# Feed-forward products summed in PSUM: one bank for p1, p6, p7, p4, another for p5, p3

## The chip, the cores and the metric

The kernel runs on one core of one Trainium2 chip. The metric is the device time of one execution in microseconds (us); lower is better. The engines are TensorE (PE in the profile; PEld is its loading of weights), VectorE (DVE), ScalarE (ACT), GpSimd (POOL) and SyncE (SP), which here only issues DMAs. Each engine and each queue works in order.

## The reference

One step of a one-layer encoder in float32: a combined input projection, two groups of attention heads, an output projection, and then a feed-forward block, for 512 prompt tokens and 8 x 16 sample tokens, 640 in all. The change touches only the feed-forward block:

```python
def merge_and_ffn(x, oa, ob, norm_grp_a, norm_grp_b, w_out, norm_ffn, w_gate, w_up, w_down):
    o = jnp.concatenate([rmsnorm(oa, norm_grp_a), rmsnorm(ob, norm_grp_b)], axis=-1)
    x = x + o @ w_out
    h = rmsnorm(x, norm_ffn)
    return x + (jax.nn.silu(h @ w_gate) * (h @ w_up)) @ w_down
```

The model width is 2048 and the inner width of the block is 5632. A final rmsnorm follows.

## The kernel before

**Precision.** Every operand is split into a high and a low part of a short float type (`split`, lines 137 to 139: ScalarE makes the high part on line 138, VectorE the low part on line 139), and a product is three matmuls (`mm3`, lines 145 to 149): high x high, high x low, low x high. One matmul has 128 x 128 weights and 320 columns, half of the 640 tokens.

**A quartet.** The three matrix products of the block use a scheme of the Strassen-Winograd kind. Two blocks of output rows by two halves of the tokens make four results c11, c21, c12, c22 of 128 x 320; seven products p1 to p7 take the place of eight. `quartet` (line 815) makes them. It loads four blocks of weights b11, b12, b21, b22 (each up to 8 x 128 columns; `get`, line 833, with the load on line 835), forms differences of them (VectorE on lines 848 and 850, GpSimd on 852 and 859) and yields one finished product after another. Each `product` (line 820) splits its weights into a pair of tiles from the list H and runs 3 x k matmuls into one PSUM bank, where k is 8 in gate and up and 5 or 6 in down. The right operands are seven sums of activations, prepared beforehand.

The results, with P for a product:

- c11 = P1 + P2
- c12 = (P1 + P6) + P5 + P3
- c22 = (P1 + P6 + P7) + P5
- c21 = (P1 + P6 + P7) + P4

Before, each product is a PSUM sum of its own: p1 and p5 lie in the two banks of one tile x, p6 and p3 in the two banks of a tile y (pool `dn`, two tiles of two banks, line 134), p7, p2 and p4 in single banks (pool `at`, four tiles of one bank, line 131). The order is p1, p6, p7, p2, p5, p4, p3. All the sums above are made by VectorE, by the helper `add` (line 869), from a bank and a tile in SBUF.

**Gate and up.** For each of 22 pairs of row blocks (line 899) there is one quartet on w_gate and one on w_up, 44 in all. ScalarE copies p1 out of PSUM (line 908), and seven adds follow (lines 910 to 921). c11 and c21 are the halves of tile y[0], c12 and c22 of y[1]. Then a gate pair is scaled and goes through SiLU (lines 931 to 933), and an up pair is multiplied by it (line 937), summed up for the down products (lines 941 to 944) and stored to `act_d` in memory (lines 945 to 947). In the first quartet (`start`) the last of the activation sums are prepared in between (`prep`); in the last (`end`) `free` gives back tiles as the products finish and fetches the first activations.

**Down.** 32 steps (`step`, line 959), each a quartet over 5 or 6 pairs; each of eight output pairs q is met four times, at t = q, q + 8, q + 16, q + 24. The results are kept in SBUF in two tiles per q, loaded with the residual. Besides, a sum u of P1 + P6 over the four visits is kept in a further tile per two q; in the last visit (`last`) it is added to c21, c22 and c12 (lines 988 to 990). That makes ten VectorE adds in a step, one less in the first eight steps, where ScalarE copies P1 to u (line 982), and three more in the last eight. Between steps the activations of a pair that comes into use are fetched and split (`fetch`, line 873: ScalarE on 881, VectorE or GpSimd on 882). Steps 30 and 31 are run in two parts: "early" (p1, p6, p7, p5, p4), in which c21 and c22 become final, then "late" (p2, p3). Between and behind them the final norm is computed (`squares`, line 1020; `rstd_steps`, line 183) and the output scaled and stored (`finish`, line 1031, with lines 1037 to 1041).

**Order.** The program is written as if each step were done in turn; a scheduler then orders each engine's queue by priority in program order and by when it expects operands to be there. So splits run one or two products ahead of the matmuls. Tiles in SBUF come from lists (S of 128 x 640, W of 128 x 1024, H taken out of W) and are handed on in the order in which they come free.

## Time and profile before

| what | value |
| --- | --- |
| median of three runs | 2685.09 us (2684.39 to 2686.73) |
| the profiled execution | 2686.44 us, of which its span 2684.7 us |
| mean granted clock of TensorE in it | 0.986 |
| VectorE adds of line 869 from a `dn` bank | 358, 163.9 us busy |
| VectorE adds of line 869 from an `at` bank | 262, 123.1 us busy |
| gate and up | from about 985 to 2085 us of the span |
| down | from about 2085 us to the end |

In a row of busy times by stretch, the first two numbers are the stretch and its length, then each engine's busy time with the count of its instructions in brackets (PE, PEld, DVE, ACT, POOL), then the granted clock of TensorE, the busy share of the DMA engines and GB/s. In a row of waits, the waiting engine with the tile and line of its instruction stands first, then what released it, then the total in us, the number of waits and the longest one. In a row of groups, the line, engine and operation, the tiles (written <- read, `dn` and `at` being PSUM), the shape and the count stand ahead of the bar, then the busy time in us and the mean in ns, then the idle time before them with its releasers. In a row of the timeline, the start and the duration in us come first.

### The profile page before, as it was taken

What the parts mean: (1) busy time and instruction counts of PE and PEld (TensorE: products, weight loads), DVE (VectorE), ACT (ScalarE), POOL (GpSimd) and SP (SyncE); (2) the same over time, 40 slices, a digit from 0 to 9 for tenths busy, and PEclk for the clock granted to TensorE, in tenths of its full rate; (3) what the DMA queues carried; (4) which work ended last, traced back from release to release, by engine and by line L of the source; (5) the groups of instructions that cost most, each with busy time, mean ns of one, the idle gap of its engine ahead of it and who ended that gap; (6) DMA issues with size and microseconds to landing.
All of it is one profiled execution on the core that took longest, in us unless ns stands there. A gap on an engine that the chain in (4) does not pass through costs nothing.

```text
span 2684.7 us, 44841 instructions
## 1 busy us (share of the span) xinstructions
PE 2602.1 (97%) x17565; PEld 2545.6 (95%) x17565; DVE 1930.3 (72%) x2956; ACT 1081.6 (40%) x1759; POOL 785.4 (29%) x564
## 2 busy tenths in 40 slices
PE   7999999999999999999999999999999999999986
PEld 7999999899899999999999999999999899999986
DVE  7565565766775787766667676667678888888897
ACT  4343343444543543333333333333334444444443
POOL 3000000001211223333333433433335534344354
PEclk8999999999999999999999999999999999999998
DMA  5222222344566433333333333333335644444344
GB/s 162 91 74 85 86 81 86 121 127 129 191 195 206 141 130 101 106 121 102 108 117 98 122 107 112 113 104 107 117 105 169 217 136 125 132 135 130 108 114 139
DMA packets 154147, 332.23 MB, mean 124 GB/s; under 512 B 18064, under 2 KB 69264, under 8 KB 153936
## 3 DMA queue, kind: packets, MB, share of 16 engines
q1 hardware_dynamic: 153936, 329.38, 38.8%
q8 instruction: 138, 2.26, 0.4%
q14 instruction: 73, 0.60, 0.1%
HBM read 274.38 MB, written 54.20 MB: 122 GB/s over the span
## 4 chain that ended last, share of the span: by engine, by line
PE 64%; DVE 5%; DMA 2%; issue 2%; ACT 1%; POOL 0%; SPq 0%; DVEq 0%; POOLq 0%; ACTq 0%
PE dn L149 13%; PE dn L147 13%; PE dn L148 13%; PE at L149 8%; PE at L148 8%; PE at L147 8%; DVE W L139 2%; DVE S L869 1%; DMA S<-act_d 1%; DMA W<-w_down 1%; DVE S L1040 1%; PE at L259 0%; DVE S L882 0%; DVE W L850 0%; ACT W L138 0%
## 5 line engine op out<-in xcount | busy, mean ns | idle before, releaser
L147 PE MATMUL dn<-S,W 128*128 128x320 f32 x3694 | 1163.5, 315 | 14.6 <-DVE S L869 5.6
L149 PE MATMUL dn<-S,W 128*128 128x320 f32 x3694 | 1154.4, 313 | 15.1 <-DVE W L139 14.9
L148 PE MATMUL dn<-S,W 128*128 128x320 f32 x3694 | 1152.7, 312 | 1.1 <-DVE S L139 1.1
L138 ACT ACTIVATE W<-W 128x1024 fp32r<-128x1024 f32 (+2 forms) x632 | 608.3, 964 | 1092.6 <-PE dn L148 553.2
L139 DVE TENSOR_TENSOR W<-W,W 128x1024 fp32r<-128x1024 f32 (+2 forms) x632 | 770.3, 1219 | 142.3 <-ACT W L138 137.5
L147 PEld LDWEIGHTS dn<-S,W 128*128 128x128 f32 x3694 | 701.9, 190 | 27.7 <-issue 10.4
L149 PEld LDWEIGHTS dn<-S,W 128*128 128x128 f32 x3694 | 701.6, 190 | 20.8 <-DVE W L139 19.6
L148 PEld LDWEIGHTS dn<-S,W 128*128 128x128 f32 x3694 | 701.6, 190 | 2.8 <-DVE S L139 1.3
L149 PE MATMUL at<-S,W 128*128 128x320 f32 x1594 | 493.6, 310 | 6.2 <-DVE W L139 6.1
L147 PE MATMUL at<-S,W 128*128 128x320 f32 x1594 | 493.0, 309 | 0.0
L148 PE MATMUL at<-S,W 128*128 128x320 f32 x1594 | 492.5, 309 | 0.0
L852 POOL TENSOR_TENSOR W<-W,W 128x1024 f32<-128x1024 f32 (+2 forms) x76 | 162.9, 2144 | 584.8 <-DVE W L139 494.6
L149 PEld LDWEIGHTS at<-S,W 128*128 128x128 f32 x1594 | 299.2, 188 | 8.6 <-DVE W L139 8.5
L147 PEld LDWEIGHTS at<-S,W 128*128 128x128 f32 x1594 | 299.6, 188 | 0.3 <-ACT W L138 0.2
L148 PEld LDWEIGHTS at<-S,W 128*128 128x128 f32 x1594 | 299.4, 188 | 0.0
L869 DVE TENSOR_TENSOR S<-S,dn 128x320 f32<-128x320 f32 x358 | 163.9, 480 | 95.7 <-PE dn L149 95.5
L848 DVE TENSOR_TENSOR W<-W,W 128x1024 f32<-128x1024 f32 (+2 forms) x76 | 134.7, 1772 | 102.0 <-DMA W<-w_up 53.1
L859 POOL TENSOR_TENSOR W<-W,W 128x1024 f32<-128x1024 f32 (+2 forms) x76 | 165.3, 2175 | 110.6 <-DVE W L139 105.5
L869 DVE TENSOR_TENSOR S<-S,at 128x320 f32<-128x320 f32 x262 | 123.1, 479 | 69.0 <-PE at L149 69.0
L218 POOL TENSOR_TENSOR S<-S,S 128x640 f32<-128x640 f32 x40 | 77.9, 1947 | 163.7 <-ACT S L217 162.9
L850 DVE TENSOR_TENSOR W<-W,W 128x1024 f32<-128x1024 f32 (+2 forms) x76 | 83.5, 1098 | 33.0 <-DMA W<-w_gate 25.3
L471 POOL MEMSET S<- 80x640 f32 x9 | 5.7, 630 | 318.9 <-PE at L155 167.1
(145 smaller groups left out, 2277.7 us busy)
## 6 DMA issues: line engine op xcount, KB each, us to landing
W<-w_gate SPq DMA_DIRECT2D x88, 512.0 KB
W<-w_up SPq DMA_DIRECT2D x88, 512.0 KB
W<-w_in SPq DMA_DIRECT2D x66, 512.0 KB
W<-w_down SPq DMA_DIRECT2D x64, 384.0 KB
W<-w_down SPq DMA_DIRECT2D x68, 320.0 KB
act_d<-S SPq DMA_DIRECT2D x66, 320.0 KB
half<-act_d SPq DMA_DIRECT2D x81, 160.0 KB
S<-act_d SPq DMA_DIRECT2D x80, 160.0 KB
```

Of the source, the lines that this page charges most:

```text
L138: self.nc.scalar.activation(hi, src, AF.Identity)
L139: self.nc.vector.tensor_tensor(lo, src, f(hi), ALU.subtract)
L147: mm(out, a[0], b[0], start=first, stop=False)
L148: mm(out, a[0], b[1], start=False, stop=False)
L149: mm(out, a[1], b[0], start=False, stop=last)
L218: (eng or nc.gpsimd).tensor_tensor(ssq, ssq, sq, ALU.add)
L848: nc.vector.tensor_tensor(b12[:, w], b12[:, w], b22[:, w], sub)
L850: nc.vector.tensor_tensor(s6[:, w], b11[:, w], b12[:, w], sub)
L852: nc.gpsimd.tensor_tensor(b11[:, w], b22[:, w], s6[:, w], sub)
L859: nc.gpsimd.tensor_tensor(b21[:, w], b21[:, w], s6[:, w], sub)
L869: add = lambda o, a, b: nc.vector.tensor_tensor(o, a, b, ALU.add)
L1040: nc.vector.scalar_tensor_tensor(t, t, gain, r_y[:, h], ALU.mult, ALU.mult)
```

## The change

`quartet` now takes two single-bank tiles x and y from pool `at`, and `product` can continue a sum that stands in a bank (`first` false: no matmul of it starts the bank anew). p1, p6, p7 and p4 are summed one after the other in x, p5 and p3 in y, and p2 has a bank alone, from pool `dn` (so has p4 of "early", and p2 and p3 of "late"). What is read from x after p6 is P1 + P6, after p7 P1 + P6 + P7, and after p4 c21 whole; what is read from y after p3 is P5 + P3. The order of the products becomes p1, p2, p6, p5, p7, p3, p4; in the first gate quartet ("lean") it is p1, p6, p7, p2, p5, p4, p3, as before; in "early" p1, p5, p6, p4, p7. b11 and b21 are loaded first, and the differences of lines 848 and 850 are formed behind p1 and p2 (behind p1 in "early"; ahead of p1 in "lean").

In gate and up, four of the seven results of a quartet are copied out by ScalarE and three are added by VectorE. In down, each result is added once (seven adds a step), in "early" p5 and p7 are added twice (seven adds for five products); u, its tiles and the three adds of the last visit are gone.

```diff
--- before.py
+++ after.py
@@ -142,11 +142,11 @@
         self.nc.scalar.activation(hi, src, AF.Identity, scale=gain)
         self.nc.vector.scalar_tensor_tensor(lo, src, gain, f(hi), ALU.mult, ALU.subtract)
 
-    def mm3(self, out, a, b, first, last):
+    def mm3(self, out, a, b, first, last, more=False):
         mm = self.nc.tensor.matmul
-        mm(out, a[0], b[0], start=first, stop=False)
-        mm(out, a[0], b[1], start=False, stop=False)
-        mm(out, a[1], b[0], start=False, stop=last)
+        mm(out, a[0], b[0], start=first, stop=False, skip_group_check=more)
+        mm(out, a[0], b[1], start=False, stop=False, skip_group_check=more)
+        mm(out, a[1], b[0], start=False, stop=last, skip_group_check=more)
 
     def mm2(self, out, a, b, first, last):
 
@@ -817,14 +817,15 @@
 
 
 
-        def product(src, which, bank):
+
+        def product(src, which, bank, first=True):
             own = n.get("H"), n.get("H")
             hl = [r(sh(x, k, P)) for x in own]
             n.split(sh(src, k, P), *hl)
             if before:
                 before(which)
             for j in range(k):
-                n.mm3(bank, (hl[0][:, j], hl[1][:, j]), lefts[j][which][1], j == 0, j == k - 1)
+                n.mm3(bank, (hl[0][:, j], hl[1][:, j]), lefts[j][which][1], first and j == 0, j == k - 1, not first)
             n.put("H", *own)
             if after:
                 after(which)
@@ -835,36 +836,72 @@
             dma(out=sh(t, k, P), in_=load(i))
             return t
 
-        w = slice(0, k * P)
-        sub = ALU.subtract
+        def minus(o, a, b, engine=nc.vector):
+            engine.tensor_tensor(o[:, :k * P], a[:, :k * P], b[:, :k * P], ALU.subtract)
+
+        alone = lambda: n.banks()[:, 0]
         if part == "late":
             b21, b22 = get(2), get(3)
             for name, src, which in (("p2", b21, 4), ("p3", b22, 6)):
-                yield name, product(src, which, n.bank()[:, :HT])
+                yield name, product(src, which, alone())
                 n.put("W", src)
             return
-        x, y = n.banks(), n.banks()
-        b12, b22, b11 = get(1), get(3), get(0)
-        nc.vector.tensor_tensor(b12[:, w], b12[:, w], b22[:, w], sub)
-        s6 = n.get("W")
-        nc.vector.tensor_tensor(s6[:, w], b11[:, w], b12[:, w], sub)
-        yield "p1", product(b11, 0, x[:, 0])
-        nc.gpsimd.tensor_tensor(b11[:, w], b22[:, w], s6[:, w], sub)
-        yield "p6", product(s6, 1, y[:, 0])
-        yield "p7", product(b12, 2, n.bank()[:, :HT])
+        x, y = (n.bank()[:, :HT] for _ in range(2))
+        b11 = get(0)
+
+        def sums():
+            b12, b22, s6 = get(1), get(3), n.get("W")
+            minus(b12, b12, b22)
+            minus(s6, b11, b12)
+            return b12, b22, s6
+
+        if part == "lean":
+            b12, b22, s6 = sums()
+            yield "p1", product(b11, 0, x)
+            minus(b11, b22, s6, nc.gpsimd)
+            yield "p6", product(s6, 1, x, False)
+            yield "p7", product(b12, 2, x, False)
+            n.put("W", b12)
+            b21 = get(2)
+            yield "p2", product(b21, 4, alone())
+            minus(b21, b21, s6, nc.gpsimd)
+            n.put("W", s6)
+            yield "p5", product(b11, 3, y)
+            n.put("W", b11)
+            yield "p4", product(b21, 5, x, False)
+            n.put("W", b21)
+            yield "p3", product(b22, 6, y, False)
+            n.put("W", b22)
+            return
+        b21 = get(2)
+        yield "p1", product(b11, 0, x)
+        if part == "early":
+            b12, b22, s6 = sums()
+            minus(b11, b22, s6, nc.gpsimd)
+            yield "p5", product(b11, 3, y)
+            n.put("W", b11, b22)
+            minus(b21, b21, s6, nc.gpsimd)
+            yield "p6", product(s6, 1, x, False)
+            n.put("W", s6)
+            yield "p4", product(b21, 5, alone())
+            n.put("W", b21)
+            yield "p7", product(b12, 2, x, False)
+            n.put("W", b12)
+            return
+        yield "p2", product(b21, 4, alone())
+        b12, b22, s6 = sums()
+        yield "p6", product(s6, 1, x, False)
+        minus(b11, b22, s6, nc.gpsimd)
+        yield "p5", product(b11, 3, y)
+        n.put("W", b11)
+        minus(b21, b21, s6, nc.gpsimd)
+        n.put("W", s6)
+        yield "p7", product(b12, 2, x, False)
         n.put("W", b12)
-        b21 = get(2)
-        if part == "all":
-            yield "p2", product(b21, 4, n.bank()[:, :HT])
-        nc.gpsimd.tensor_tensor(b21[:, w], b21[:, w], s6[:, w], sub)
-        n.put("W", s6)
-        yield "p5", product(b11, 3, x[:, 1])
-        n.put("W", b11)
-        yield "p4", product(b21, 5, n.bank()[:, :HT])
+        yield "p3", product(b22, 6, y, False)
+        n.put("W", b22)
+        yield "p4", product(b21, 5, x, False)
         n.put("W", b21)
-        if part == "all":
-            yield "p3", product(b22, 6, y[:, 1])
-        n.put("W", b22)
 
     add = lambda o, a, b: nc.vector.tensor_tensor(o, a, b, ALU.add)
     prep = prepare([5, 6, 7], [7])
@@ -903,22 +940,15 @@
             y = n.get("S"), n.get("S")
             c11, c21, c12, c22 = y[0][:, :HT], y[0][:, HT:], y[1][:, :HT], y[1][:, HT:]
             start, end = i == 0 and src == "w_gate", i == NPAIR - 1 and src == "w_up"
-            for step, bank in quartet(8, load, hs, (lambda w: next(prep)) if start else None, free if end else None):
-                if step == "p1":
-                    nc.scalar.activation(c11, bank, AF.Identity)
-                elif step == "p6":
-                    add(c12, c11, bank)
-                elif step == "p7":
-                    add(c21, c12, bank)
-                elif step == "p5":
-                    add(c22, c21, bank)
-                    add(c12, c12, bank)
-                elif step == "p2":
-                    add(c11, c11, bank)
-                elif step == "p4":
-                    add(c21, c21, bank)
-                elif step == "p3":
-                    add(c12, c12, bank)
+            into = {"p1": c11, "p2": c11, "p6": c12, "p3": c12, "p5": c22, "p7": c22, "p4": c21}
+            copied = ("p1", "p6", "p7" if start else "p5", "p4")
+            for step, bank in quartet(8, load, hs, (lambda w: next(prep)) if start else None, free if end else None,
+                                      "lean" if start else "all"):
+                c = into[step]
+                if step in copied:
+                    nc.scalar.activation(c, bank, AF.Identity)
+                else:
+                    add(c, c, bank)
             if start:
                 for _ in prep:
                     pass
@@ -959,7 +989,7 @@
     def step(t, part="all"):
         now = active(t)
         nxt = active(t + 1) if t + 1 < STEPS else []
-        cnt, q, last = len(now), t % 8, t >= STEPS - 8
+        cnt, q = len(now), t % 8
 
         def after(which):
             n.put("S", *(lefts[j][which][0] for j in now if j not in nxt))
@@ -970,36 +1000,17 @@
             x, y = n.get("S"), n.get("S")
             dma(out=x, in_=x2_d[q])
             dma(out=y, in_=x2_d[q + 8])
-            sums.append((x, y, n.get("S") if q % 2 == 0 else sums[-1][2]))
-        x, y, u = sums[q]
+            sums.append((x, y))
+        x, y = sums[q]
         c11, c21, c12, c22 = x[:, :HT], x[:, HT:], y[:, :HT], y[:, HT:]
-        us = u[:, HT * (q % 2):HT * (q % 2) + HT]
+        into = {"p1": [c11], "p2": [c11], "p6": [c12], "p5": [c22], "p7": [c22], "p3": [c12], "p4": [c21]}
+        if part == "early":
+            into["p5"], into["p7"] = [c22, c12], [c22, c21]
         o = 2 * sum(len(active(i)) for i in range(q, t, 8))
         load = lambda z: io["w_down"][q + 8 * (z % 2), :, o + cnt * (z // 2):o + cnt * (z // 2) + cnt]
         for name, bank in quartet(cnt, load, [lefts[j] for j in now], None, after, part):
-            if name == "p1":
-                if t < 8:
-                    nc.scalar.activation(us, bank, AF.Identity)
-                else:
-                    add(us, us, bank)
-                add(c11, c11, bank)
-            elif name == "p6":
-                add(us, us, bank)
-                if last:
-                    for c in (c21, c22, c12):
-                        add(c, c, us)
-            elif name == "p7":
-                add(c21, c21, bank)
-                add(c22, c22, bank)
-            elif name == "p5":
-                add(c22, c22, bank)
-                add(c12, c12, bank)
-            elif name == "p2":
-                add(c11, c11, bank)
-            elif name == "p4":
-                add(c21, c21, bank)
-            elif name == "p3":
-                add(c12, c12, bank)
+            for c in into[name]:
+                add(c, c, bank)
             yield name
 
     def run(*args):
```

## The prediction

> **What bounds the kernel now.** I read the busy table first, then TensorE's matmuls stretch by stretch, then, where it does not keep its pace, what it waits for.
>
> ```profile
> PE 2602.1 (97%) x17565; PEld 2545.6 (95%) x17565; DVE 1930.3 (72%) x2956; ACT 1081.6 (40%) x1759; POOL 785.4 (29%) x564
> ```
>
> ```profile
> 960.00:1030.00 70.00, 63.92 (x414) 62.11 (x413) 56.41 (x70) 32.36 (x50) 22.64 (x10) 0.95 0.32 104
> 1030.00:2060.00 1030.00, 1030.00 (x7024) 1030.00 (x7024) 711.91 (x756) 356.38 (x381) 388.99 (x212) 1.00 0.34 111
> 2060.00:2130.00 70.00, 60.10 (x375) 57.29 (x374) 61.65 (x85) 36.09 (x72) 38.71 (x32) 0.95 0.70 230
> 2130.00:2230.00 100.00, 97.68 (x665) 97.18 (x664) 84.95 (x127) 46.07 (x79) 40.11 (x30) 1.00 0.51 149
> 2230.00:2530.00 300.00, 300.00 (x2048) 300.00 (x2047) 255.44 (x348) 127.85 (x195) 119.04 (x78) 1.00 0.46 128
> 2530.00:2650.00 120.00, 106.43 (x664) 101.82 (x664) 111.82 (x158) 56.00 (x96) 64.44 (x41) 0.96 0.40 113
> ```
>
> The second row is nearly the whole gate/up stage: 7024 matmuls in 1030 us, 0.1466 us each, TensorE never idle, the granted clock 1.00. That is the floor; the down steps hold it too from 2230 to 2530 (300 / 2048 = 0.1465). The change keeps every matmul, so it can gain only where a row holds fewer matmuls than its length allows. Length minus count times 0.1466: 960 to 1030 loses 9.3 us, 2060 to 2130 loses 15.0, 2130 to 2230 loses 2.5, 2530 to 2650 loses 22.7. Together 49.5 us is all there is.
>
> What ends TensorE's waits at the first down steps (2060 to 2130), then in the last ones (2530 to 2650), and what VectorE does in the latter:
>
> ```profile
> PE dn L149 <- DVE W L139: 4.4, 4, 1.6
> PE dn L147 <- ACT S L881: 3.5, 1, 3.5
> PE dn L147 <- DVE S L869: 1.7, 2, 1.1
> ...
> PE at L149 <- DVE W L139: 5.8, 6, 1.7
> PE dn L147 <- DVE S L869: 4.0, 3, 2.3
> PE dn L149 <- DVE W L139: 3.4, 3, 2.4
> ...
> L139 DVE TENSOR_TENSOR W<-W,W 128x640 fp32r<-128x640 f32 x47 | 55.0, 1170 | 1.2 <-ACT W L138 0.9
> L869 DVE TENSOR_TENSOR S<-S,dn 128x320 f32<-128x320 f32 x41 | 18.4, 475 | 1.5 <-PE dn L149 1.5
> L869 DVE TENSOR_TENSOR S<-S,S 128x320 f32<-128x320 f32 x21 | 15.2, 773 | 0.0
> L869 DVE TENSOR_TENSOR S<-S,at 128x320 f32<-128x320 f32 x29 | 13.3, 476 | 2.2 <-PE at L149 2.2
> ```
>
> From 2530 every wait of TensorE ends on VectorE, which is busy 111.8 of 120 us: there it is the bound. TensorE waits for the low half of split weights (L139) and for a bank that an add (L869) has not read. 47 us of VectorE's time in this stretch are adds of line 869.
>
> **The change part by part.** *Adds removed in gate/up.* Of seven VectorE adds a quartet keeps three; the other four become three more ScalarE copies from PSUM.
>
> ```profile
> L869 DVE TENSOR_TENSOR S<-S,dn 128x320 f32<-128x320 f32 x167 | 77.3, 484 | 76.4 <-PE dn L149 76.3
> L869 DVE TENSOR_TENSOR S<-S,at 128x320 f32<-128x320 f32 x126 | 60.8, 482 | 55.4 <-PE at L149 55.4
> L908 ACT ACTIVATE S<-dn 128x320 f32<-128x320 f32 x42 | 17.6, 419 | 0.0
> ```
>
> VectorE loses 44 x 4 x 0.483 = 85 us, ScalarE gains 44 x 3 x 0.419 = 55 us. VectorE was busy 69% of this stage and ScalarE 35% (the second window row) beside a full TensorE, so I book zero. If the cover went (ScalarE late with a copy), the next product on that bank would wait; it comes a whole product of 24 x 0.1466 = 3.5 us later, and ScalarE's other work is a single weight split at a time.
>
> *Adds removed in the last down steps.* The window 2530 to 2650 holds the triple adds of seven steps (21 rows, S from S), which vanish, and from five full steps three more adds each (ten become seven), from the two early ones one each (eight become seven): 17 x 0.475 = 8.1. With the 15.2 that is 23.3 us off 111.8, leaving 88.5 us of VectorE beside 664 x 0.1466 = 97.3 us of TensorE, 91%. Between 2230 and 2530 VectorE is 85% busy and TensorE loses nothing; so at 91% some loss stays. Bounds: all 22.7 us come back, or, if the splits are late for loads and ScalarE and not for VectorE's length, only the waits on L869, 4.0. I take 14, nearer to the upper end, because the releaser rows above name VectorE alone. What is late next is the load behind L848 and the squares of the norm.
>
> *First down steps.* The last up quartet loses four adds and each step of the first eight loses two: up to four steps here, so 10 or 12 adds, about 5 us, against 17.5 us lost from 2060 to 2230. The longest wait, 3.5, ends on ScalarE's split of a fetched activation, behind DMA. SyncE's in-order queue has a long wait of its own there, and the matmuls after TensorE's long wait come further apart:
>
> ```profile
> SPq L945 <- DVE S L937: 6.2, 1, 6.2
> ...
> 2088.18 0.47 PE L147 MATMUL dn<-S,W 128*128 128x320 f32 x1
> 2088.45 0.47 PE L148 MATMUL dn<-S,W 128*128 128x320 f32 x1
> ```
>
> The store of c11 waits for the product of L937, which takes all of tile y[0]; that tile now gets its last value, c21, from the last product p4 instead of the last but one. So this store, and any load put behind it in the queue, can be a product later (3.5 us), and the fetches with it. I take -4, between -9 (the waits on L139 and L869, 6.1, and what they cost in clock) and +4. On the clock: after the 3.5 us wait matmuls start 0.27 apart (2088.18, 2088.45) instead of 0.147; some 15 of them cost 1.8 us more. The Trainium skill, "TensorE: Matmul & The Clock Gate", section "What's actually happening", says that the clock is halved after an idle window and returns after a busy one; the trace agrees, 0.27 against 0.147. By it alone a wait of 3.5 cut short would give 5.3 us and not 3.5; I keep both sizes inside the bounds above.
>
> *The first gate quartet ("lean").* p1, p6 and p7 follow each other on one bank, so TensorE twice stands still while ScalarE copies: from the start of the last matmul 0.31 to its end (0.15 of it would be waited anyway), 0.42 for the copy (L908), and some 0.15 back to TensorE (an add that ends at 2107.85 below releases the matmul at 2108.00). About 0.8 each, 1.6 in all, 3.7 if a split of 1.06 stands ahead each time. Four adds less give VectorE 1.9 there. The norm's three banks now come from the pool of x and y: 0 to 1 more. Net 0, between -2 and +3.
>
> ```profile
> 2107.38 0.47 DVE L869 TENSOR_TENSOR S<-S,dn 128x320 f32<-128x320 f32 x1
> ...
> 2108.00 0.38 PE L147 MATMUL dn<-S,W 128*128 128x320 f32 x1 [1.12 <-DVE S L869]
> ```
>
> *The added wait.* Before, a product's bank was not written again for several products. Now x takes p6 after p1, p7 after p6, p4 after p7, with one other product between (18 x 0.1466 = 2.64 us in a down step of six); a read later than that stops TensorE, and behind it the whole in-order queue of products. No row of before shows this wait. The nearest is one step's reads:
>
> ```profile
> 2333.60 0.31 PE L147 MATMUL at<-S,W 128*128 128x320 f32 x1
> ...
> 2333.66 2.63 DVE L848 TENSOR_TENSOR W<-W,W 128x768 f32<-128x768 f32 x1 [0.75 <-DMA W<-w_down]
> 2336.21 0.47 DVE L869 TENSOR_TENSOR S<-S,dn 128x320 f32<-128x320 f32 x1
> 2336.61 1.24 DVE L139 TENSOR_TENSOR W<-W,W 128x768 fp32r<-128x768 f32 x1
> 2337.77 0.87 DVE L869 TENSOR_TENSOR S<-S,at 128x320 f32<-128x320 f32 x2
> ...
> 2336.24 0.31 PE L147 MATMUL at<-S,W 128*128 128x320 f32 x1
> ```
>
> p6 ends about 2333.76 (0.16 after p7 starts); its add sits behind the weight difference L848 and ends at 2336.68, 2.92 later: 0.28 too late by the new rule, some 0.4 with the way back. p7 ends at 2336.40 and its two adds at 2338.64, 2.24 later, in time. So one hand-off of three is late in such a step. The change also moves L848: p1 and p2 no longer need the differences, so they run one product further ahead, and the three adds less a step clear the queue. Bounds: 0, and 30 steps x 0.4 = 12. I take +3, nearer to 0, since the deciding add is late only because of L848.
>
> The early steps end on p7 with two adds instead of one before the squares of the norm: +0.4. The rows behind the last product (scaling and stores) are untouched.
>
> Sum: 0 - 14 - 4 + 0 + 3 + 0.4 = -14.6. The profiled execution took 2686.4 with its span of 2684.7; the median shown is 2685.1. 2686.4 - 14.6 = 2671.8; I say **2672**.
>
> **The rivals.** *The hand-off stalls (slower).* If in the down steps all three hand-offs come 0.4 late, because VectorE's adds stand behind L848, L850 and splits that GpSimd's work stretches (the 2.63 above), 30 x 3 x 0.4 = 36 us are added in place of my 3: 2686.4 - 18 + 0.4 + 36 = 2705; with two of three, 2693. It decides from 18 + 5.4 = 23 us, 0.26 per hand-off. For it: the 2.92 above, and VectorE at 85%. Against it: the differences move away from these adds. The Trainium skill, "PSUM — Partial Sum Buffer", section "PSUM bank collisions raise a hardware error", says that two engines must not be in one bank at once and that hardware does not arbitrate; by it the wait must be a semaphore and can't be shortened. No run here shows a collision.
>
> *Nothing moves.* VectorE's time in the last steps goes, but the splits still come late since ScalarE, the fetches and the loads set them; then only the 4.0 of L869 comes back and the hand-offs take it: 2686.4 - 4 + 3 = 2685. For it: over the whole run a load of weights ends VectorE's wait before L848, 28 times in the down steps. Against: the releasers above.
>
> ```profile
> DVE W L848 <- DMA W<-w_down: 25.4, 28, 2.0
> ```
>
>
> *More comes back.* All 22.7, and 9 at the first steps, no hand-off late: 2686.4 - 31.7 = 2655.
>
> **How the numbers follow.** Forecast 0.52, more 0.12, nothing 0.18, hand-offs 0.18. Forecast's own range: 2663 to 2681. The range for 8 in 10 reaches from between the forecast and the case of more to the two-of-three case: 2657 to 2694. About 0.2% (5.4 us) is what a measurement of this kernel can tell from no change: faster 0.64, same 0.18, slower 0.18.
>
> **What would show it.** Right: VectorE falls by some 140 us and ScalarE rises by about 52 (8 x 0.42 of first-step copies go); 1030 to 2060 still runs at 0.1466 a matmul; the last 120 us before the tail lose 5 to 12 us instead of 22.7 and L869 from S alone is gone. Wrong: TensorE waiting on L869 or on the copy at the first matmul of p6, p7 or p4 in most steps (the hand-off), or waits on L139 in the last steps as long as before (VectorE's length was not the cause), or a longer wait on L881 at the first step (the store behind c21).

## The result and the profile after

The changed kernel takes 2760.0 us (median of four runs, 2753.9 to 2764.6) against 2685.9 for the kernel before in the same comparison (2684.4 to 2688.2). The ratio is 1.0274, with a 95% interval of 1.0250 to 1.0297: 74 us slower. The forecast was 2672, in a range of 2657 to 2694. The profiled execution of the changed kernel took 2764.6 us. One execution of all the runs below, one of four of `e9_all_fix_half`, took 5258 us and is left out of that kernel's time and ratio.

First the busy table of the changed kernel, then two of its costliest groups, from its profile page:

```profile
PE 2624.7 (95%) x17565; PEld 2550.1 (92%) x17565; DVE 1923.2 (70%) x2672; ACT 1112.3 (40%) x1883; POOL 796.8 (29%) x564
...
L139 DVE TENSOR_TENSOR W<-W,W 128x1024 fp32r<-128x1024 f32 (+2 forms) x632 | 830.4, 1314 | 221.1 <-ACT W L138 216.8
...
L961 DVE TENSOR_TENSOR S<-S,S 128x640 f32<-128x640 f32 x44 | 121.5, 2764 | 4.1 <-ACT S L205 3.4
```

VectorE has 284 instructions fewer (2956 to 2672), but is busy only 7 us less and not 140: what remains got longer. The split's low half took 1219 ns on average before (770.3 us in 632, on the page of before) and takes 1314; the scaling ahead of SiLU, line 931 before and 961 now, goes from 1277 ns (53.6 us in 42, in the stretch 1030 to 2060 of before) to 2764 (over the whole run).

TensorE stretch by stretch in the changed kernel; the last row is the 120 us that stand as far from the end as 2530 to 2650 did before:

```profile
960.00:1030.00 70.00, 61.02 (x381) 58.95 (x381) 52.14 (x63) 32.29 (x52) 21.30 (x10) 0.90 0.29 97
1030.00:2060.00 1030.00, 1000.88 (x6739) 988.02 (x6738) 711.96 (x561) 372.77 (x482) 382.91 (x201) 1.00 0.32 105
...
2608.00:2728.00 120.00, 102.49 (x642) 99.63 (x643) 84.43 (x115) 51.97 (x90) 57.12 (x39) 0.94 0.37 107
```

Gate and up, which lost nothing, now hold 6739 matmuls in 1030 us instead of 7024: 285 x 0.1466 = 41.8 us lost in the stage that I had booked at zero. The last 120 us before the tail lose 120 - 642 x 0.1466 = 25.9 us, as before (22.7), though VectorE fell there from 111.8 to 84.4 us.

What TensorE waits for, over the whole run (two rows), from 1030 to 2060 (one), and in those last 120 us (three):

```profile
PE at L147 <- ACT S L949: 37.3, 38, 4.6
PE at L147 <- DVE S L906: 27.9, 27, 2.7
...
PE at L147 <- ACT S L949: 28.2, 33, 1.9
...
PE at L147 <- DVE S L906: 12.5, 8, 2.7
PE at L147 <- ACT S L918: 4.3, 1, 4.3
PE at L149 <- DVE W L139: 0.6, 2, 0.3
```

Line 949 is ScalarE's copy out of a bank, line 906 VectorE's add from one, and the waiting instruction is on `at`, where x and y now lie: the hand-off of a bank within a sum. Counting matmuls behind p2 places the 33 waits on line 949 in gate and up: 18 (20.3 us) are at p6 of an up quartet, 15 (8.0 us) at p7 of a gate quartet. The rows hold 28.2 of the 41.8 us lost; in the passage below a stall costs some 0.2 us more than its row, which would make 7 us more, an estimate, and the rest is not traced. In the last steps the waits on the split's low half have gone, from 5.8 + 3.4 to 0.6, as forecast; the hand-off, 12.5, and a fetch, 4.3, stand in their place.

**The stall in gate and up, seen once.** From the timeline of the changed kernel, engine by engine (TensorE, ScalarE, VectorE, GpSimd):

```profile
1590.50 0.31 PE L147 MATMUL at<-S,W 128*128 128x320 f32 x1
1590.94 0.31 PE L147 MATMUL dn<-S,W 128*128 128x320 f32 x1
...
1594.02 0.31 PE L147 MATMUL dn<-S,W 128*128 128x320 f32 x1
1595.82 0.41 PE L147 MATMUL at<-S,W 128*128 128x320 f32 x1 [1.20 <-ACT S L949]
...
1588.09 0.74 ACT L962 ACTIVATE S<-S 128x640 f32<-128x640 f32 x1 [3.27 <-DVE S L961]
...
1594.70 0.74 ACT L962 ACTIVATE S<-S 128x640 f32<-128x640 f32 x1 [4.60 <-DVE S L961]
1595.35 0.42 ACT L949 ACTIVATE S<-at 128x320 f32<-128x320 f32 x1
...
1585.31 2.75 DVE L961 TENSOR_TENSOR S<-S,S 128x640 f32<-128x640 f32 x1
...
1591.64 3.04 DVE L961 TENSOR_TENSOR S<-S,S 128x640 f32<-128x640 f32 x1
...
1584.96 2.42 POOL L840 TENSOR_TENSOR W<-W,W 128x1024 f32<-128x1024 f32 x1 [12.46 <-DVE W L139]
...
1590.60 3.39 POOL L840 TENSOR_TENSOR W<-W,W 128x1024 f32<-128x1024 f32 x1
```

The up quartet's p1 gives way to p2, on `dn`, at 1590.94. From about 1591.1 the copy of p1 could run, and p6, next on that bank, is due when p2 ends. But the copy starts at 1595.35. Ahead of it in ScalarE's queue stands the SiLU of the gate pair's tile that is scaled second (line 962). ScalarE stood still for 4.60 us until VectorE had scaled that tile, 1591.64 to 1594.68; the scaling ran beside GpSimd's weight difference. p2 covers 3.5 us of that, and p6 starts 1.20 us late by the row (1.4 late by TensorE's pace). ScalarE's own waits, from 1030 to 2060, before (first row) and after (second fence):

```profile
ACT S L932 <- DVE S L931: 37.2, 41, 1.9
```

```profile
ACT S L962 <- DVE S L961: 153.2, 40, 4.6
```

The wait of SiLU on the scaling existed before and hurt nobody, since no product was due on p1's bank for several products.

**The stall in down, seen once.** The timeline of the changed kernel again, TensorE and then VectorE:

```profile
2407.82 0.31 PE L149 MATMUL at<-S,W 128*128 128x320 f32 x1
2409.43 0.39 PE L147 MATMUL at<-S,W 128*128 128x320 f32 x1 [1.29 <-DVE S L906]
...
2403.62 0.96 DVE L139 TENSOR_TENSOR W<-W,W 128x768 fp32r<-128x768 f32 x1 [0.24 <-ACT W L138]
2407.92 0.96 DVE L840 TENSOR_TENSOR W<-W,W 128x768 f32<-128x768 f32 x1 [3.34 <-DMA W<-w_down]
2408.80 0.48 DVE L906 TENSOR_TENSOR S<-S,at 128x320 f32<-128x320 f32 x1
```

VectorE stands still for 3.34 us at a weight difference of the next step, whose load has not come; p5's add is queued behind it, ends at 2409.28, and p3, which goes on in p5's bank, starts at 2409.43. Between 2110 and 2620, placed by counting matmuls behind p2 again, 8 of the 18 waits on an add are at p3 (9.1 us), 9 at p4 (6.8), one at p7 (0.9) and none at p6.

### The profile page after: what moved, and what is told of

The parts are those of the page before. It is cut to its first block, busy times and chain, and to the rows that moved or that the text cites. A ratio compares the mean times of both kernels' runs of the same rounds, so it can differ in the third digit from the quotient of the medians.

```text
span 2762.8 us, 44735 instructions
## 1 busy us (share of the span) xinstructions
PE 2624.7 (95%) x17565; PEld 2550.1 (92%) x17565; DVE 1923.2 (70%) x2672; ACT 1112.3 (40%) x1883; POOL 796.8 (29%) x564
## 5 line engine op out<-in xcount | busy, mean ns | idle before, releaser
L147 PE MATMUL at<-S,W 128*128 128x320 f32 x3148 | 988.3, 314 | 76.1 <-ACT S L949 37.3
L139 DVE TENSOR_TENSOR W<-W,W 128x1024 fp32r<-128x1024 f32 (+2 forms) x632 | 830.4, 1314 | 221.1 <-ACT W L138 216.8
L149 PE MATMUL at<-S,W 128*128 128x320 f32 x3148 | 978.3, 311 | 3.1 <-DVE W L139 3.1
L148 PE MATMUL at<-S,W 128*128 128x320 f32 x3148 | 978.2, 311 | 1.3 <-DVE S L139 1.3
L147 PEld LDWEIGHTS at<-S,W 128*128 128x128 f32 x3148 | 595.8, 189 | 100.6 <-ACT S L949 49.3
L147 PE MATMUL dn<-S,W 128*128 128x320 f32 x2140 | 678.3, 317 | 1.4 <-DVE S L326 0.9
L149 PE MATMUL dn<-S,W 128*128 128x320 f32 x2140 | 668.0, 312 | 7.9 <-DVE W L139 7.9
L148 PE MATMUL dn<-S,W 128*128 128x320 f32 x2140 | 668.0, 312 | 0.0
L149 PEld LDWEIGHTS at<-S,W 128*128 128x128 f32 x3148 | 595.6, 189 | 4.3 <-DVE W L139 4.3
L148 PEld LDWEIGHTS at<-S,W 128*128 128x128 f32 x3148 | 596.0, 189 | 1.8 <-DVE S L139 1.8
L840 POOL TENSOR_TENSOR W<-W,W 128x1024 f32<-128x1024 f32 (+2 forms) x152 | 348.4, 2293 | 748.0 <-DVE W L139 671.9
L147 PEld LDWEIGHTS dn<-S,W 128*128 128x128 f32 x2140 | 406.6, 190 | 11.4 <-issue 5.2
L149 PEld LDWEIGHTS dn<-S,W 128*128 128x128 f32 x2140 | 405.9, 190 | 10.6 <-DVE W L139 9.5
L148 PEld LDWEIGHTS dn<-S,W 128*128 128x128 f32 x2140 | 406.3, 190 | 1.5
L840 DVE TENSOR_TENSOR W<-W,W 128x1024 f32<-128x1024 f32 (+2 forms) x152 | 168.8, 1111 | 208.0 <-DMA W<-w_up 100.0
L919 POOL TENSOR_TENSOR S<-S,S 128x320 fp32r<-128x320 f32 x102 | 125.1, 1233 | 186.1 <-ACT S L918 178.2
L961 DVE TENSOR_TENSOR S<-S,S 128x640 f32<-128x640 f32 x44 | 121.5, 2764 | 4.1 <-ACT S L205 3.4
L918 ACT ACTIVATE S<-S 128x320 fp32r<-128x320 f32 x189 | 83.9, 462 | 75.2 <-DMA S<-act_d 64.8
```

The source lines that it names most:

```text
L139: self.nc.vector.tensor_tensor(lo, src, f(hi), ALU.subtract)
L147: mm(out, a[0], b[0], start=first, stop=False, skip_group_check=more)
L148: mm(out, a[0], b[1], start=False, stop=False, skip_group_check=more)
L149: mm(out, a[1], b[0], start=False, stop=last, skip_group_check=more)
L840: engine.tensor_tensor(o[:, :k * P], a[:, :k * P], b[:, :k * P], ALU.subtract)
L918: nc.scalar.activation(hi, raw, AF.Identity)
```

## The experiments

My theory after this reading: two hand-offs cost the time, each through an in-order queue. In gate and up the copy of p1 stands behind a SiLU that waits for VectorE; in down an add stands behind a weight difference that waits for its load. The rivals: that VectorE's longer operations cost the time by themselves, that the new order of loads does, and that the sums in PSUM cannot be covered in so few banks whatever the order of the queues.

**Halves of the change.** `quartet_old` is the quartet of before; `e1_gu_new` uses it with the step of before in down, and `e2_down_new` with the adds of before in gate and up.

```diff
-        for name, bank in quartet(cnt, load, [lefts[j] for j in now], None, after, part):
+        for name, bank in quartet_old(cnt, load, [lefts[j] for j in now], None, after, part):
```

> Gate and up as changed, down as before. Between 1030 and 2060 us the changed kernel runs 285 matmuls fewer than before (42 us), and some 5 us more go in the first quartet. If stalls of the two stages add up, this kernel takes about 2686 + 46 = 2732 us, and its waits on the ScalarE copies (L949) stay about 37 us. Rival (the loss sits in the passage from one stage to the other, or in the down steps): below 2705.

> Gate and up as before, down as changed. By adding up: 2686 + 28 = 2714 us, with TensorE waiting on adds from PSUM (L906) some 26 us in down and on no ScalarE copy. If the shorter VectorE work of the last steps pays as I predicted, and only gate and up lose: 2672.

Gate and up alone: 2743.8 us, ratio 1.0218 [1.0203, 1.0233], +59.3 on the 2684.5 of before in that comparison. Down alone: 2704.3, ratio 1.0068 [1.0051, 1.0085], +19.8. Together 79, near the 74 of the whole. TensorE's longest sum of waits in the first kernel, then in the second (lines 1003 and 960 are the copy and the add there):

```profile
PE at L147 <- ACT S L1003: 38.5, 40, 4.4
```

```profile
PE at L147 <- DVE S L960: 27.7, 29, 3.3
```

The windows of `e1_gu_new`, then of `e2_down_new` (its last one begins 20 us later than in before, as the end does):

```profile
960.00:1030.00 70.00, 60.41 (x374) 58.88 (x373) 51.27 (x63) 31.52 (x51) 21.81 (x10) 0.90 0.28 94
1030.00:2060.00 1030.00, 998.78 (x6725) 986.01 (x6724) 714.21 (x559) 371.80 (x480) 382.09 (x200) 1.00 0.32 105
```

```profile
2060.00:2130.00 70.00, 59.27 (x366) 56.98 (x366) 63.15 (x79) 34.69 (x69) 42.28 (x33) 0.93 0.69 224
2130.00:2230.00 100.00, 94.07 (x630) 92.17 (x629) 80.98 (x107) 41.80 (x70) 38.29 (x28) 1.00 0.50 147
2230.00:2530.00 300.00, 292.90 (x1972) 288.92 (x1971) 238.99 (x285) 123.38 (x189) 117.92 (x76) 1.00 0.43 126
...
2550.00:2670.00 120.00, 102.81 (x650) 99.69 (x649) 83.55 (x116) 51.88 (x89) 58.18 (x39) 0.96 0.36 106
```

Matmuls missing against before, times 0.1466: in gate and up 40 at the start (5.9 us) and 299 (43.8); the other 10 lie behind 2060. In down 44 from 2060 to 2230 (6.5), 76 from 2230 to 2530 (11.1), 14 in the last 120 us (2.1), which is the 19.8.

**The copy's place in gate and up.** Two edits on the changed kernel: SiLU and what goes with it written behind p1's copy of the up quartet (`issue_after` keeps it behind that copy on ScalarE), and a tile of its own for p6's copy, which otherwise waits for a result tile that is still being stored. `e3_gu_fix` has both, `e5_scratch6` only the second, `e6_silu_behind` only the first.

```diff
+                if step == "p1" and src == "w_up":
+                    with n.tc.issue_after(nc.cur_bb.bb.instructions[-1]):
+                        for z in gate:
+                            nc.vector.tensor_tensor(z, z, r_f, ALU.mult)
+                            nc.scalar.activation(z, z, AF.Silu)
+                            nc.gpsimd.tensor_tensor(z, z, r_f, ALU.mult)
...
-                if step in copied:
+                if step == "p6" and not start:
+                    held = n.scratch()
+                    nc.scalar.activation(held, bank, AF.Identity)
+                elif step == "p3" and not start:
+                    add(c, held, bank)
+                elif step in copied:
```

> The changed kernel with two orders mended in gate and up, same matmuls: p6's copy goes to a scratch tile and is added to the result at p3 (so it needs no free result tile), and the gate pair's SiLU is queued behind the copy of p1 of the up quartet. If the 29 us that TensorE waits on L949 between 1030 and 2100 come from these two queues, this kernel takes 2760 minus about 38 = 2722, and 1030 to 2060 holds over 6950 matmuls. Rival (weights come late, or VectorE and GpSimd slow each other): at least 2750.

> Only the first of the two orders mended in the run before (e3): p6's copy goes to a scratch tile. It takes away the waits of an up-to-gate passage, where the copy waits for a result tile that the pair before still stores. By the waits on L949 of the changed kernel, which come about 0.4 us each at this place and 1.2 us at the other, it gives a third of e3's 46 us: 2760 - 15 = 2745. Rival (each of the two feeds the other, so that one alone gives next to nothing or nearly all): over 2755 or under 2722.

> Only the second: the gate pair's SiLU stands behind the copy of p1 of the up quartet on ScalarE. It takes away the waits of a gate-to-up passage: 2760 - 30 = 2730, with some 21 waits of about 0.4 us on L949 left. Rival as in the run before it.

Both: 2713.7 us, 1.0109 [1.0094, 1.0124]. The tile alone: 2759.4, 1.0262 [1.0245, 1.0279], no gain, a miss. The order alone: 2716.5, 1.0104 [1.0084, 1.0124], 43 us below the changed kernel. So the edit of the order is nearly all of it. `e6_silu_behind`: the gate/up window, then its timeline at the passage from a gate quartet to its up quartet (ScalarE, VectorE, GpSimd):

```profile
1030.00:2060.00 1030.00, 1029.63 (x7018) 1029.06 (x7017) 703.20 (x586) 394.43 (x502) 365.17 (x210) 1.00 0.34 109
```

```profile
1617.62 0.42 ACT L949 ACTIVATE S<-at 128x320 f32<-128x320 f32 x1
1618.45 1.37 ACT L956 ACTIVATE S<-S 128x640 f32<-128x640 f32 x2 [0.42 <-DVE S L955]
...
1610.46 2.73 DVE L955 TENSOR_TENSOR S<-S,S 128x640 f32<-128x640 f32 x1
...
1615.39 3.03 DVE L955 TENSOR_TENSOR S<-S,S 128x640 f32<-128x640 f32 x1
...
1610.11 2.40 POOL L840 TENSOR_TENSOR W<-W,W 128x1024 f32<-128x1024 f32 x1 [13.14 <-DVE W L139]
1614.41 3.32 POOL L840 TENSOR_TENSOR W<-W,W 128x1024 f32<-128x1024 f32 x1 [1.90 <-DVE W L139]
```

7018 matmuls: the floor is back, and TensorE waits on line 949 once in these 1030 us, for 0.3 us; the waits at p7 of the gate quartets are gone too, though nothing was edited there. In the passage shown the scaling still takes 2.73 and 3.03 us beside GpSimd, and TensorE does not wait, as p1's copy now stands ahead of SiLU. This passage is not the usual one, though: the edit also moved the second scaling, which in 17 of the 20 whole passages of this stretch runs clear of GpSimd and takes 0.81 us (shortest, median and longest in ns, first and second scalings together):

```profile
L955 DVE TENSOR_TENSOR S<-S,S x41: 811/2255/3037, 1067.5 to 2054.7; 128x640 f32<-128x640 f32 x41
```

In the two other passages where it is as long, from 1319.82 and from 2009.75, TensorE does not wait either. So the order is enough by itself in three passages, and in the other 17 it comes together with a short scaling. A short scaling might have been enough as well: in the passage of the changed kernel shown above, 0.81 us from 1591.64, SiLU (0.74) and the copy (0.42) would have read the bank by about 1593.6, before the end of p2 at about 1594.5. That is an estimate; no run shortens the scaling alone.

**The differences in down.** `e4_diffs_behind` is the changed kernel with VectorE's two differences kept behind p7's add of the step before.

```diff
-            minus(b12, b12, b22)
-            minus(s6, b11, b12)
+            with (n.tc.issue_after(gate_ins[0]) if gate_ins[0] is not None else contextlib.nullcontext()):
+                minus(b12, b12, b22)
+                minus(s6, b11, b12)
...
+            if name == "p7":
+                gate_ins[0] = nc.cur_bb.bb.instructions[-1]
```

> The changed kernel with one order mended in down: the two VectorE weight differences of a step are queued behind the add of p7 of the step before. Same work, same loads. If the reads of p5 and p7 come late because a difference stands ahead of them waiting for its load, the waits on L906 in down fall from about 26 us to under 8 and the kernel takes 2760 - 18 = 2742. Rival (the reads are late because VectorE as a whole is behind, or the differences are needed that early): no gain, or the waits move to the weight splits (L139) and it takes 2760 or more.

2748.2 us, 1.0242 [1.0220, 1.0264]: 12 us below the changed kernel, where I expected 18; the intervals of the two overlap. In mid-down, first the changed kernel's window, then that of this experiment:

```profile
2300.00:2560.00 260.00, 253.91 (x1714) 251.08 (x1713) 204.05 (x246) 106.37 (x162) 104.74 (x66) 1.00 0.43 127
```

```profile
2300.00:2560.00 260.00, 259.12 (x1764) 258.42 (x1763) 224.02 (x254) 108.92 (x169) 104.60 (x69) 1.00 0.43 128
```

Fifty matmuls more, 7.3 us, in these steps, which are then 1.4 us from the floor. So the place of the differences is what cost them. In down as a whole TensorE's waits on adds only fall from 27.6 us in 26 waits to 14.5 in 17, and not under 8; those that stay lie ahead of 2300 and behind 2560, most of them at p6.

**All three edits, and what is left.** `e7_all_fix` has the three; `e8_all_fix_start` also has the first gate quartet as it was before; `e9_all_fix_half` lets a fetch take a tile from the list S only when more than seven are free, instead of three.

```diff
-            for step, bank in quartet(8, load, hs, (lambda w: next(prep)) if start else None, free if end else None,
-                                      "lean" if start else "all"):
+            if start:
+                for step, bank in quartet_old(8, load, hs, (lambda w: next(prep)) if start else None, free if end else None):
...
-            if len(n.lists["S"]) > 3:
+            if len(n.lists["S"]) > 7:
```

> Both orders in gate and up (e3, 46 us) and the differences behind p7's add in down (e4, 12 us). If the two stages add up: 2760 - 58 = 2702. Waits on L906 left at the passages, about 15 us. Rival (mending one stage moves its stall to the other): over 2710.

> As e7, and the first gate quartet made as before the change (own banks, sums on VectorE). From 980 to 1030 us the changed kernel runs 245 matmuls and before 277. If the two hand-offs without a product between them cost that: 32 x 0.1466 = 4.7 us less than e7. Rival (the start is bound by the activation sums either way): within 2 us of e7.

> e7 with one number changed: a fetch takes a second S tile for its raw activations only if more than 7 S tiles are free in place of 3. Without u four S tiles more are free, so that the changed kernel takes an S tile for all of these loads and before took the two small scratch tiles for 81 of them. If the loads that hold up ScalarE (L922 behind S<-act_d, 80 us idle in e7) come late because those S tiles are still in use, the waits at the passages shrink and the kernel takes 2705 - 8 = 2697. Rival (the loads are late by their place in SyncE's queue or by the pair that comes into use): 2705, within 3 us.

2705.2 us, 1.0063 [1.0048, 1.0078]: the two causes add up. It differs from `e3_gu_fix` (1.0109 [1.0094, 1.0124]) by the place of the differences alone, so their gain is clear of the noise here. The other two are misses: 2704.7 (1.0064 [1.0049, 1.0079]) and 2706.7 (1.0069 [1.0051, 1.0087]). With the first quartet as before the start still loses its time: 960 to 1030 holds 372 matmuls, 381 in `e7_all_fix` and 414 in the kernel before. TensorE's longest wait there, in `e8_all_fix_start` (line 140 is the split's low half), comes in the second quartet, between two groups of small matmuls of the norm (lines 192 and 204); the last row is the first matmul of a product behind them:

```profile
1009.45 1.39 PE L192 MATMUL at<-cst,S 128*128 128x1 f32 x12
...
1014.70 0.42 PE L150 MATMUL dn<-S,W 128*128 128x320 f32 x1 [3.16 <-DVE W L140]
...
1020.13 0.61 PE L148 MATMUL at<-S,W 128*128 128x320 f32 x1
```

So "lean" is not what costs the start its 5 us. From 1009.45 to 1020.13 TensorE makes only 7 matmuls of the products, all of p2. The third waits for the low half of p2's split, which takes 3.17 us beside GpSimd's weight difference (1011.22 to 1013.56). In the kernel before, a split there is as long (3.25 us), but the 24 matmuls of p1 cover it: from 1011.81 to 1020.65 TensorE makes 29. So the stretch is 1.8 us longer and holds 22 matmuls fewer (3.2 us), 5 us in all. In the changed kernel it lies at 1015.43 to 1025.08 and holds 7 too. Why p1 comes behind the norm there stays open. It would fit that p1 and the norm now take banks of the same pool, which no run tests.

**Was VectorE's length the cause in the last steps?** Two kernels from before: `e10_before_u_pool` gives the 24 adds of u in the last visit to GpSimd, `e12_before_no_u3` leaves these adds, and with them that part of the result, out.

```diff
                 if last:
                     for c in (c21, c22, c12):
-                        add(c, c, us)
+                        nc.gpsimd.tensor_tensor(c, c, us, ALU.add)
```

> The kernel before with only the 24 adds of u to c21, c22 and c12 in the last visit put on GpSimd in place of VectorE: 15 us of VectorE's work less between 2530 and 2650, nothing else changed, no bank read in between. If VectorE's length is what costs TensorE 22.7 us there, as I predicted, about two thirds of my 14 come back: 2686 - 9 = 2677. Rival (the stall comes from loads and fetches that hold ScalarE and VectorE in order, not from the sum of VectorE's work): within 4 us of 2686, or slower, since the adds are slower on GpSimd and p7's add waits for them.

> The kernel before without the 24 adds of u to c21, c22 and c12 in the last visit (the output lacks that part): 15 us of VectorE's work less between 2530 and 2650 and none more on GpSimd, so a clean form of e10. If VectorE's length costs TensorE its 22.7 us there, 9 to 14 come back: 2673 to 2677. Rival (the fetches that hold ScalarE, and the order behind them, set those waits): at least 2682.

On GpSimd: 2686.4 us, 0.9993 [0.9984, 1.0002], a miss. Left out: 2674.7, 0.9955 [0.9942, 0.9969], 12.2 us faster. Their last 120 us, in that order:

```profile
2530.00:2650.00 120.00, 103.08 (x667) 98.95 (x666) 106.49 (x136) 56.30 (x96) 85.55 (x62) 0.99 0.40 113
```

```profile
2530.00:2650.00 120.00, 113.91 (x755) 109.26 (x754) 108.64 (x152) 61.05 (x105) 65.00 (x43) 1.00 0.40 114
```

On GpSimd the adds shorten VectorE by 5 us (111.8 to 106.5) and not by the 15.2 that they took, since what remains gets longer (the split's low half of 128x640 from 1194 to 1276 ns on average). Besides, VectorE now waits 7.4 us for GpSimd's adds (line 990):

```profile
L869 DVE TENSOR_TENSOR S<-S,at 128x320 f32<-128x320 f32 x25 | 12.0, 481 | 7.4 <-POOL S L990 7.4
```

Left out, the stretch takes 755 matmuls and loses 9.3 us instead of 22.7. So these adds on VectorE did cost about what I said; whether by their length or by their place in its queue, no run separates.

**What holds the last steps of the repaired kernel.** `e13_all_fix_no_sq` is `e7_all_fix` without the squares for the final norm in these steps, except the first, so its norm is not the reference's.

```diff
-            for i in range(2):
-                n.add_square(ssq, sums[t % 8][i], t == STEPS - 8 and i == 0, "S")
+            if t == STEPS - 8:
+                n.add_square(ssq, sums[t % 8][0], True, "S")
```

> e7 without the squares of the final norm in steps 24 to 29 but the first (the norm of the output lacks them): ScalarE loses 11 squares of 0.74 us, GpSimd 11 sums of 1.9 us, and the tiles of the squares are free for fetches. If the waits of the last steps (about 19 us from 2550 to 2662 in e7, the longest behind L922) come from fetches that wait for tiles held by those sums, they halve: 2705 - 9 = 2696. Rival (hand-offs and loads alone): 2705, within 3 us.

2688.9 us, 1.0009 [1.0000, 1.0018]: 16 us below `e7_all_fix` (14.5 by the ratios), more than I expected. The last steps, and ScalarE's wait for a fetched activation (line 922 there) from 2500 to 2660, first in `e7_all_fix` (two fences), then here:

```profile
2540.00:2660.00 120.00, 101.92 (x653) 99.20 (x651) 94.06 (x116) 54.54 (x94) 61.98 (x42) 0.96 0.36 108
```

```profile
ACT S L922 <- DMA S<-act_d: 38.8, 12, 6.7
```

```profile
2540.00:2660.00 120.00, 113.19 (x750) 111.43 (x749) 97.11 (x135) 54.09 (x89) 39.20 (x27) 0.97 0.35 102
```

```profile
ACT S L922 <- DMA S<-act_d: 15.6, 12, 3.8
```

The fetches come late while the squares hold tiles of the same list S and GpSimd adds them up (62.0 us of GpSimd against 39.2). The 11 squares fewer on ScalarE are in the gain too; whether the tiles, GpSimd's time or ScalarE's matters most was not told apart. The kernel before computes these squares as well.

**A better version?** `e11_best_try` takes the gate and up of before, the changed down with the differences behind, and the fetch threshold of `e9_all_fix_half`.

> Gate and up as before the change, down as changed with the differences behind p7's add (e4) and the fetches' tiles as in e9. If the parts add up: 2704 (e2) - 12 (e4) - 4 to 8 (e9) = about 2686, level with before. Rival (the passages keep their waits): 2692 or more.

2698.3 us, 1.0047 [1.0034, 1.0059], a miss: 6 us below `e2_down_new` and not 16 to 20. No version of the change that I found comes below the kernel before.

## Why the prediction was wrong

*What bounds the kernel.* Right: the floor of 0.1466 us a matmul, and that only rows below it can gain. The other half I had not drawn: a stage that stands at the floor can only lose, so a new wait in it has to be priced there first.

*Adds removed in gate/up, zero.* This step failed: +59 in place of 0 (`e1_gu_new`), most of the miss. I priced the added wait only in down, and dismissed it here with the sentence that "ScalarE's other work is a single weight split at a time". ScalarE also holds SiLU, which waits for VectorE. In the new order c21 comes with the last product, p4, so the scaling and SiLU of its tile fall into the time of p1 and p2 of the up quartet, beside GpSimd's difference, and p1's copy stands behind them. Putting the copy ahead gave 43 us back (`e6_silu_behind`). The 85 us that VectorE was to lose in the stage did not show either: it is busy 712.0 us from 1030 to 2060, as before (711.9), because its remaining operations got longer.

*The last down steps, -14.* That VectorE's work there costs TensorE time, and how much, was borne out: 12.2 us by `e12_before_no_u3`, and VectorE came to 84.4 us where I had worked out 88.5. But the gain did not come. The failed part is "what is late next". I named a load and the squares; the load and the fetches did come late, and the hand-off with them, and the stretch loses 25.9 us as against 22.7.

*First down steps, -4.* Wrong in sign: +6.5 in `e2_down_new`. The fewer adds are there, but TensorE waits 7.5 us on adds in these two stretches, 1.7 before.

*The first gate quartet, 0.* The forecast for "lean" stands: undoing it changed nothing. The start's 5 us lie in the second quartet, around the norm. If they come from the norm's banks, my 0 to 1 for these was too small; no run tests that.

*The added wait in down, +3.* Mis-sized: TensorE waited 27.7 us on adds, 29 times, in `e2_down_new`. I had taken one hand-off in three to be 0.4 late, because only L848 made it late and the change moved L848 forward. That move made it worse: ahead of its load, the difference holds VectorE's queue for up to 3.7 us (26.9 us in 13 waits between 2300 and 2560; before, 11.8 us in 14 waits, 1.4 at most):

```profile
DVE W L840 <- DMA W<-w_down: 26.9, 13, 3.7
```

A late hand-off is late by 1 us on average then (27.7 / 29), and not by 0.4; their number, 29, is about that of my upper bound (30 x 0.4 = 12), of which I took a quarter. I also counted three hand-offs a step, on x, and left out the fourth, p5 to p3 on y, which is the one shown above and has 9.1 of the 16.8 us of waits placed there.

*The rivals.* The hand-off was the right rival. That down alone landed at 2704, where it was priced at 2705, is partly luck: the rival put 36 us of waits, 90 of 0.4, against a gain of 18; measured were 27.7 us in 29 waits and no gain. Its place was too narrow, since it was asked of down and not of gate and up. The signal named for it came, though not in most steps: TensorE waits at p6 and p7 in gate and up, and in down at p4 and also at p3, which was not named.

*The rule against it.* The Trainium skill, "Perfetto Trace Analysis", section "Matmuls", says that independent matmul groups should rotate through PSUM banks, so that the reading of one overlaps the next. The trace agrees: four products in one bank with a read between each turned a stage without a wait into one that waits 33 times on line 949 in 1030 us. With the copy put ahead in its queue the same four products in one bank wait once there (`e6_silu_behind`): it counts whether the reading is done within the product that stands in between.

*Open:* why p1 comes behind the norm at the start, the hand-offs that stay at the first down steps in `e7_all_fix`, whether a shorter scaling alone would have kept gate and up at the floor, and what in the squares holds the fetches.

## What to carry to other kernels

Where a buffer is handed on sooner, list for every reader of it what stands ahead of it in its engine's in-order queue, and what that in turn waits for; a reader behind an instruction that waits for another engine or for a load is as late as that is. Do this first in the stage that runs at its floor, since it has only time to lose. Fewer instructions on the busiest engine are worth what the windows say only if no one waits anew for those that remain.

## What the hardware showed besides

A VectorE multiply of two SBUF tiles (128x640) that starts while GpSimd subtracts two others ends 0.68 or 0.69 us after GpSimd does. In the changed kernel 1588.06 follows 1587.38 and 1594.68 follows 1593.99; in `e6_silu_behind` 1613.19 follows 1612.51 and 1618.42 follows 1617.73. Of the 44 multiplies of line 961 in the changed kernel 42 start beside GpSimd, and all 42 end so; the other two take 0.82 and 0.83 us. In the kernel before, 42 of 44 do the same, but start later in GpSimd's operation and so take 1277 ns on average and not 2764. So it looks not slowed but held until GpSimd is done. The Trainium skill, "SBUF — State Buffer", section "Who interferes with whom", says this: a VectorE operation with two SBUF inputs and a GpSimd operation that reads SBUF share a pair of ports, and the later one is blocked until the other ends. The trace agrees in all of these cases. It is likely part of why moving 24 adds to GpSimd bought nothing; the 7.4 us that VectorE then waited for them are another part, and no run separates the two.
